# Weight remainders by an accumulating DMA instead of a VectorE subtraction, in a two-layer fp32 trunk

## The chip, the core and the metric

The kernel runs on one core of one Trainium2 chip. The metric is the time of one execution on the device in microseconds, as the median of the runs. Beside it stands one execution taken by the hardware profiler, from which all rows below come.

## The reference, cut to what matters

A two-layer backbone over 256 latent tokens `x` and 256 context tokens `ctx`, 1024 channels wide. Each layer is a half-step SwiGLU feed-forward block, a token mixer of four parallel branches (gated MLP, convolution, bidirectional mLSTM, pooling) with a gated merge, and a second feed-forward block. Shift, scale and gate of each step come from `w_ada`. In the last layer the context is dropped once the mixer has read it.

```python
def swiglu_ffn(h, w_in, w_out):
    a = h @ w_in
    return (jax.nn.silu(a[..., :D_FF]) * a[..., D_FF:]) @ w_out

for l in range(DEPTH):
    ...
    x = residual(x, swiglu_ffn(modulate(x, mod_x, 0), ffn_w_in[l, 0], ffn_w_out[l, 0]), ...)
    h_ctx = residual(h_ctx, swiglu_ffn(modulate(h_ctx, mod_c, 0), ...), ...)
    ...
    y_x, _, _ = token_mixer(modulate(x, mod_x, 1), lw, st_f, st_b)
    x = residual(x, y_x, mod_x, 1, ln_g[l, 1], ln_b[l, 1], 1.0)
    x = residual(x, swiglu_ffn(modulate(x, mod_x, 2), ffn_w_in[l, 1], ffn_w_out[l, 1]), ...)
```

All weights and activations are fp32, and the products have to come out close to fp32.

## The kernel before, in words

Channels lie on the 128 partitions and tokens in the columns: columns 0 to 255 are the context, 256 to 511 the latent tokens, so most matmuls are 512 columns wide, and 256 wide once only the latent tokens are left (second mixer for the most part, and the last feed-forward block).

Each fp32 product is made of three matmuls in a shorter format (`F32R`). A value is split into a high part `hi`, the value rounded to that format, and a remainder `lo`, the value minus `hi`. `mm3` then issues `hi`·`xh`, `hi`·`xl` and `lo`·`xh` into one PSUM tile, in this order: the remainder of a weight is first wanted at the third matmul of a chunk.

`wload` brings in one chunk of weights. SyncE's queue loads it from HBM into a buffer `raw` (128 partitions x 1024 fp32, 512 KiB; 768 columns and 384 KiB for the first part of each feed-forward block's `ffn_out`). `split` has ScalarE write `hi` (line 129) and VectorE write `lo` as `raw` minus `hi` (line 130). There are four `raw` buffers, six `hi` and six `lo`. The `raw` buffers are shared with the rows of `w_ada` (`mods`, line 213, and `start`, line 350), of which VectorE makes two dot products each. `wload` serves the feed-forward blocks (`ffn_tiles`, `out_tiles`), and through `chunk` all projections and the merge of the mixer. Two chunks are split by calls of `split` of their own and not through `wload`: one pair of the first chunks (line 520) and the small gate weights (line 896).

A feed-forward block goes over 22 column blocks in three parts (`PARTS`): for each block two chunks of `ffn_in`, a SiLU on ScalarE, a product on VectorE and a split of the result; after each part eight chunks of `ffn_out` (768 columns wide in the first part). Between the steps of a part, `pump` inserts dot products for the modulation of later steps (`PUMPS`): up to three dot products for each column block or output chunk, none in the last feed-forward block. The mixer inserts work of its branches between projections by the costs that `counted` and `mm` add up.

The engines' instructions are ordered by the tile framework from data dependences and free buffers, so a chunk may be loaded and split before the program text comes to it, as far as buffers are free. GpSimd has some additions at the start (line 375) and memsets of the edges of padded tiles.

Of the kernel before, what the change touches and what calls it, by code (L numbers as in the profile page):

```python
# [10 lines left out]
F32 = mybir.dt.float32  # L11
F32R = mybir.dt.float32r
AF = mybir.ActivationFunctionType
ALU = mybir.AluOpType
# [46 lines left out]
def trunk_kernel(ctx: ExitStack, tc: tile.TileContext, I: dict, out: bass.AP):  # L61
# [11 lines left out]
    def nm(s):  # L73
        uid[0] += 1
        return f"{s}{uid[0]}"
# [27 lines left out]
    V, S, G_ = nc.vector, nc.scalar, nc.gpsimd  # L103
# [6 lines left out]
    def counted(f, fix, per):  # L110
        def g(*a, **k):
            work["v"] += fix + per * size(k["out"] if "out" in k else a[0])
            return f(*a, **k)  # L113
        return g

    tt, stt = (counted(f, 70, 1.05) for f in (V.tensor_tensor, V.scalar_tensor_tensor))
    ts, scan = counted(V.tensor_scalar, 70, 0.55), counted(V.tensor_tensor_scan, 70, 1.05)
# [6 lines left out]
    def act(o, i, f, **kw):  # L124
        S.activation(o, i, f, **kw)  # L125

    def split(hi, lo, src, scale=None):
        if scale is None:
            act(hi, src, AF.Copy)
            tt(out=lo, in0=src, in1=hi.bitcast(F32), op=ALU.subtract)  # L130
        else:
            act(hi, src, AF.Copy, scale=scale)
            stt(out=lo, in0=src, scalar=scale, in1=hi.bitcast(F32), op0=ALU.mult, op1=ALU.subtract)

    def wload(ap, n=1024):
        raw = wp.tile([128, 1024], F32, tag="raw", name=nm("raw"), bufs=4)
        nc.sync.dma_start(raw[:, :n], ap)
        hi = wp.tile([128, 1024], F32R, tag="hi", name=nm("hi"), bufs=6)
        lo = wp.tile([128, 1024], F32R, tag="lo", name=nm("lo"), bufs=6)
        split(hi[:, :n], lo[:, :n], raw[:, :n])  # L140
        return hi, lo

    def mm3(ps, wh, wl, xh, xl, start, stop):
# [359 lines left out]
    def ffn_tiles(l, w, js):  # L503
        tiles = []
        for j in js:
            for h in range(2):
                wh, wl = wload(I["ffn_in"][l, w, j, h])
                tiles.append((mmb(), wh, wl))
        return tiles
# [14 lines left out]
    def ffn(l, w, bd, first, cs, order, np_, nm_=1):  # L524
# [5 lines left out]
        for pi, (j0, j1) in enumerate(PARTS):  # L530
# [26 lines left out]
            def evac(m, p, c, vs):  # L557
                resid(m, p, l, s, vs)
                if fin:
                    nrm.arrive(m, c)  # L560
                pump(nm_)

            rest = out_tiles(lambda m: wload(I["ffn_out"][l, w, m, :, j0 * 128:j1 * 128], (j1 - j0) * 128),
                             gh, gl, cs, order, evac, LAG if fin and len(order) > 1 else 0)
        return nrm, rest
# [8 lines left out]
    def mixer(l, bd, cs, sets, order):  # L574
# [46 lines left out]
        def chunk(key):  # L621
            n = plan.index(key)
            for x in plan[n:n + 1 + AHEAD]:
                if x not in ready:
                    w = I["w_" + x[0]][l]
                    w = w[x[1] // 4, x[1] % 4] if x[0] == "br" else w[x[1]]
                    if plain(x):
                        ready[x] = wp.tile([128, 1024], F32, tag="raw", name=nm("raw"), bufs=4)
                        nc.sync.dma_start(ready[x], w)
                    else:  # L630
                        ready[x] = wload(w)
            pump()
            return ready[key]
# [688 lines left out]
```

## Time and profile before

| | |
|---|---|
| median of 3 runs | 2267.71 us (2266.44 to 2270.55) |
| the profiled execution's own time | 2267.27 us |
| its span | 2265.5 us, 31565 instructions |
| TensorE busy | 2221.0 us (98%) |
| VectorE busy | 1630.0 us (72%) |
| ScalarE busy | 947.0 us (42%) |
| GpSimd busy | 19.9 us (1%) |
| loads, SyncE's queue | 321.22 MB, 43.9% of 16 engines' span |

The span runs from the first to the last instruction; the run's own time has a little around it. Busy time is that in which an engine executed an instruction; the DMA share is the mean busy share of the core's 16 DMA engines. In the rows, `out<-in` names tiles of the program without their buffer numbers, and a line such as L113 or L122 may be a helper's, which records all operations of its kind.

### The profile page before, as it was taken

The numbers are of one execution on the slowest core, as the hardware profiler recorded it, in microseconds if no ns is written. First come the engines' busy times: TensorE is split into PE (matmuls) and PEld (weight loads), VectorE is DVE, ScalarE is ACT, GpSimd is POOL, SyncE is SP. The second block draws the span as 40 slices with busy tenths as digits, with TensorE's granted clock in tenths as the row PEclk, the third lists the DMA queues.
The fourth block names the chain that finished last, engine by engine and source line by source line (L and its number), as shares of the span: only waits on it lengthen the run. The fifth ranks groups of instructions, "written<-read, shape, count | busy, mean of one in ns | idle before, by whom it ended". The sixth has DMA issues, their size and how long they took to land.

```text
span 2265.5 us, 31565 instructions
## 1 busy us (share of the span) xinstructions
PE 2221.0 (98%) x12216; PEld 1908.4 (84%) x12216; DVE 1630.0 (72%) x2881; ACT 947.0 (42%) x1477; POOL 19.9 (1%) x82
## 2 busy tenths in 40 slices
PE   7999999999999999999999999999999999998997
PEld 4888788988888888898888888888889998998997
DVE  6998855768995754795746498766558988776656
ACT  5323123742345753362222254222226645755443
POOL 2000000000000000000000000000000000000000
PEclk9999999999999999999999999999999999999999
DMA  8676643223232132244545425554434543354652
GB/s 308 220 229 221 192 152 94 98 84 113 94 99 88 57 103 93 96 135 150 170 129 158 130 84 186 179 180 152 140 102 142 192 139 103 122 174 136 203 180 83
DMA packets 94454, 323.23 MB, mean 143 GB/s; under 512 B 10592, under 2 KB 12640, under 8 KB 94304
## 3 DMA queue, kind: packets, MB, share of 16 engines
q1 hardware_dynamic: 94304, 321.22, 43.9%
q8 instruction: 96, 1.57, 0.3%
q14 instruction: 54, 0.44, 0.1%
HBM read 320.12 MB, written 1.05 MB: 142 GB/s over the span
## 4 chain that ended last, share of the span: by engine, by line
PE 87%; DVE 7%; DMA 3%; issue 2%; ACT 2%; SPq 0%; DVEq 0%; ACTq 0%
PE mm L122 82%; DVE junk L216 2%; DMA ada<-in_wada 1%; DVE lo L113 1%; PE num L122 1%; DMA raw<-in_ffn_in 1%; DVE junk L366 1%; ACT hi L125 1%; DVE ah L113 0%; PE gt L122 0%; PE ax L122 0%; PE qk L122 0%; PE bcm L122 0%; PE bcr L122 0%; PE st L122 0%
## 5 line engine op out<-in xcount | busy, mean ns | idle before, releaser
L125 ACT ACTIVATE hi<-raw 128x1024 fp32r<-128x1024 f32 (+1 forms) x462 | 474.5, 1031 | 1040.0 <-PE mm L122 659.1
L122 PE MATMUL mm<-xh,hi 128*128 128x512 f32 (+1 forms) x2448 | 847.8, 349 | 5.0 <-ACT hi L125 3.0
L122 PE MATMUL mm<-xl,hi 128*128 128x512 f32 (+1 forms) x2448 | 850.0, 348 | 0.0
L122 PE MATMUL mm<-xh,lo 128*128 128x512 f32 (+1 forms) x2448 | 850.0, 348 | 0.0
L113 DVE TENSOR_TENSOR lo<-raw,hi 128x1024 fp32r<-128x1024 f32 (+1 forms) x462 | 546.2, 1185 | 264.6 <-ACT hi L125 262.4
L122 PEld LDWEIGHTS mm<-xh,hi 128*128 128x128 f32 x2448 | 462.4, 190 | 65.0 <-ACT hi L125 4.4
L122 PEld LDWEIGHTS mm<-xh,lo 128*128 128x128 f32 x2448 | 464.8, 190 | 58.8 <-DVE lo L113 0.4
L122 PEld LDWEIGHTS mm<-xl,hi 128*128 128x128 f32 x2448 | 465.2, 190 | 57.9 <-issue 0.7
L122 PE MATMUL mm<-gh,hi 128*128 128x512 f32 (+1 forms) x1600 | 405.8, 344 | 5.6 <-ACT gh L125 4.7
L216 DVE CUSTOM_DVE_ANT_0 junk<-ada,cbc 128x1024 bf16<-128x1024 f32 x256 | 312.9, 1222 | 107.1 <-DMA ada<-in_wada 104.0
L122 PEld LDWEIGHTS mm<-gh,hi 128*128 128x128 f32 x1600 | 276.6, 189 | 48.0 <-ACT gh L125 5.1
L122 PE MATMUL mm<-gh,lo 128*128 128x512 f32 (+1 forms) x800 | 275.5, 345 | 0.0
L122 PEld LDWEIGHTS mm<-gh,lo 128*128 128x128 f32 x800 | 150.8, 189 | 20.2 <-issue 0.7
L113 DVE SCALAR_TENSOR_TENSOR ah<-mm,gate,ah 128x256 f32<-128x256 f32 x192 | 86.4, 479 | 81.4 <-PE mm L122 81.2
L113 DVE SCALAR_TENSOR_TENSOR cacc<-pd,cw,cacc 128x512 f32<-128x512 f32 (+1 forms) x240 | 133.1, 613 | 0.2
L122 PE MATMUL mm<-yh,hi 128*128 128x512 f32 (+1 forms) x512 | 129.3, 339 | 0.1
L113 DVE TENSOR_TENSOR sg<-sg,mm 128x512 f32<-128x512 f32 (+1 forms) x87 | 53.7, 618 | 82.4 <-PE mm L122 81.7
L122 PEld LDWEIGHTS mm<-yh,hi 128*128 128x128 f32 x512 | 88.0, 189 | 11.6 <-ACT yh L125 0.3
L122 PE MATMUL mm<-yh,lo 128*128 128x512 f32 (+1 forms) x256 | 86.5, 338 | 0.0
L125 ACT ACTIVATE gh<-sg 128x512 fp32r<-128x512 f32 (+1 forms) x88 | 50.5, 574 | 76.0 <-DVE sg L113 75.5
L122 PE MATMUL mm<-mh,hi 128*128 128x256 f32 (+1 forms) x320 | 67.0, 306 | 0.5 <-ACT mh L125 0.3
L125 ACT ACTIVATE xf<-ah,bp,gp 128x256 f32<-128x256 f32 x88 | 48.8, 592 | 21.6 <-DVE ah L113 16.5
(241 smaller groups left out, 1759.6 us busy)
## 6 DMA issues: line engine op xcount, KB each, us to landing
raw<-in_ffn_in SPq DMA_DIRECT2D x176, 512.0 KB, 3.4
ada<-in_wada SPq DMA_DIRECT2D x136, 512.0 KB, 4.2
raw<-in_ffn_out SPq DMA_DIRECT2D x64, 512.0 KB, 3.7
raw<-in_w_G SPq DMA_DIRECT2D x64, 512.0 KB, 3.3
raw<-in_w_br SPq DMA_DIRECT2D x32, 512.0 KB, 3.3
raw<-in_ffn_out SPq DMA_DIRECT2D x32, 384.0 KB, 3.4
raw<-in_w_o SPq DMA_DIRECT2D x24, 512.0 KB, 3.4
shw<-in_wshift SPq DMA_DIRECT2D x16, 256.0 KB, 5.8
```

The lines of the kernel that those rows point to most:

```text
L113: return f(*a, **k)
L122: nc.tensor.matmul(o, w, x, **kw)
L125: S.activation(o, i, f, **kw)
L216: V.tensor_tensor_reduce(out=cur["junk"], in0=w, in1=cur["c"][:, v], scale=1.0, scalar=0.0, op0=ALU.mult, op1=ALU.add, accum_out=m[:, v, t ...
L366: V.tensor_tensor_reduce(out=cur["junk"], in0=w, in1=cur["c"][:, v], scale=1.0, scalar=0.0, op0=ALU.mult, op1=ALU.add, accum_out=m[:, v, k ...
```

## The change: what it does

In `wload` alone, the call of `split` is replaced by three instructions: ScalarE writes `hi` as before, VectorE multiplies `hi` by -1 into `lo`, and GpSimd's queue issues a DMA that adds `raw` to `lo` in place, both in SBUF. The other uses of `split` stay.

```diff
         nc.sync.dma_start(raw[:, :n], ap)
         hi = wp.tile([128, 1024], F32R, tag="hi", name=nm("hi"), bufs=6)
         lo = wp.tile([128, 1024], F32R, tag="lo", name=nm("lo"), bufs=6)
-        split(hi[:, :n], lo[:, :n], raw[:, :n])
+
+        act(hi[:, :n], raw[:, :n], AF.Copy)
+        ts(out=lo[:, :n], in0=hi[:, :n].bitcast(F32), scalar1=-1.0, scalar2=None, op0=ALU.mult)
+        G_.dma_start(lo[:, :n], raw[:, :n], accum_op=ALU.add)
         return hi, lo
```

`act` is an activation on ScalarE, `ts` a `tensor_scalar` on VectorE, `G_` is GpSimd. Nothing else in the kernel differs.

## Rows read from the trace of the kernel before

**Rows 1.** The page: busy times, DMA queue, and the chain that ended last
```profile
PE 2221.0 (98%) x12216; PEld 1908.4 (84%) x12216; DVE 1630.0 (72%) x2881; ACT 947.0 (42%) x1477; POOL 19.9 (1%) x82
...
q1 hardware_dynamic: 94304, 321.22, 43.9%
...
PE 87%; DVE 7%; DMA 3%; issue 2%; ACT 2%; SPq 0%; DVEq 0%; ACTq 0%
```

**Rows 2.** Windows, stages A to G: busy time per engine, clock, DMA share, GB/s
```profile
0.00:300.00 300.00, 281.47 (x1200) 219.60 (x1201) 252.18 (x426) 96.72 (x138) 12.05 (x18) 0.98 0.70 230
300.00:985.00 685.00, 683.65 (x3438) 571.01 (x3438) 481.11 (x873) 306.31 (x493) 4.05 (x35) 1.00 0.29 95
985.00:1675.00 690.00, 689.58 (x3276) 575.89 (x3276) 450.11 (x725) 225.03 (x315) 0.13 (x1) 1.00 0.47 149
1675.00:1760.00 85.00, 84.86 (x639) 79.72 (x638) 71.62 (x145) 50.51 (x93) 0.73 (x10) 1.00 0.40 134
1760.00:1880.00 120.00, 115.83 (x815) 108.53 (x815) 111.67 (x218) 64.75 (x97) 2.25 (x8) 1.00 0.50 161
1880.00:2060.00 180.00, 171.90 (x1263) 161.63 (x1264) 142.37 (x314) 110.94 (x207) 0.67 (x10) 0.96 0.43 137
2060.00:2232.00 172.00, 171.84 (x1418) 171.09 (x1418) 98.60 (x132) 83.76 (x123) 0.00 (x0) 0.99 0.55 172
```

**Rows 3.** The same windows for tile lo alone: PE, PEld, DVE, POOL
```profile
0.00:300.00 300.00, 140.25 (x357) 67.89 (x357) 61.18 (x52) 0.00 (x0) 0.98 0.70 230
300.00:985.00 685.00, 374.68 (x1014) 190.57 (x1014) 134.65 (x114) 0.95 (x1) 1.00 0.29 95
985.00:1675.00 690.00, 403.11 (x1079) 202.70 (x1079) 155.69 (x131) 0.00 (x0) 1.00 0.47 149
1675.00:1760.00 85.00, 58.14 (x199) 37.52 (x198) 23.18 (x19) 0.00 (x0) 1.00 0.40 134
1760.00:1880.00 120.00, 80.63 (x265) 50.05 (x265) 41.86 (x38) 0.95 (x1) 1.00 0.50 161
1880.00:2060.00 180.00, 104.06 (x354) 68.08 (x354) 55.97 (x46) 0.00 (x0) 0.96 0.43 137
2060.00:2232.00 172.00, 134.13 (x473) 90.95 (x473) 71.34 (x61) 0.00 (x0) 0.99 0.55 172
```

**Rows 4.** Groups of VectorE by form: count, busy us, mean ns, idle before
```profile
L113 DVE TENSOR_TENSOR lo<-raw,hi 128x1024 fp32r<-128x1024 f32 x422 | 514.5, 1222 | 250.1 <-ACT hi L125 248.0
L113 DVE TENSOR_TENSOR lo<-raw,hi 128x768 fp32r<-128x768 f32 x32 | 30.6, 955 | 14.5 <-ACT hi L125 14.4
L113 DVE TENSOR_SCALAR lf<-lf,cols 64x512 f32<-64x512 f32 x2 | 0.9, 474 | 0.0
L113 DVE TENSOR_SCALAR gate<-gate 128x16 f32<-128x16 f32 x4 | 0.7, 174 | 0.1
```

**Rows 5.** Windows, the first 57 us, columns as in Rows 2
```profile
0.00:57.00 57.00, 43.87 (x175) 25.73 (x176) 39.45 (x79) 30.33 (x58) 12.05 (x18) 0.97 0.87 306
```

**Rows 6.** Waits of SyncE's queue: us in total, times, longest
```profile
SPq L137 <- DVE lo L113: 1167.1, 304, 20.8
```

**Rows 7.** Tile raw: durations in ns (min/median/max), and its loads' landing
```profile
L125 ACT ACTIVATE hi<-raw x462: 213/1061/1101, 21.3 to 2234.2; 128x1024 fp32r<-128x1024 f32 x142, 128x768 fp32r<-128x768 f32 x10, 128x32 fp32r<-128x32 f32 x2
...
L137 SPq DMA_DIRECT2D raw<-in_ffn_in x174: 327/328/328, 12.5 to 2201.2; - x174
...
DMA to landing us min/median/max: 2.1/3.4/7.7
```

**Rows 8.** Waits of ScalarE, the longest in total
```profile
ACT hi L125 <- PE mm L122: 659.1, 228, 7.1
```

**Rows 9.** Timeline of TensorE at the start: start, duration, the first matmul with lo
```profile
24.38 0.63 PE L122 MATMUL mm<-xh,lo 128*128 128x512 f32 x1
```

**Rows 10.** Stage A for tile ada alone: VectorE busy (x), clock, DMA share
```profile
0.00:300.00 300.00, 151.53 (x122) 0.98 0.70 230
```

## The prediction

> **What bounds the kernel now.** I read the page's busy shares first. TensorE is busy 98% of the span and the chain of work that ended last is 87% TensorE; GpSimd is nearly empty [rows 1]. So little is there to be won (2265.5 - 2221.0 = 44.5 us), and the question is what the change can make TensorE wait for.
>
> Then I cut the span into stages and read the windows, because the change adds transfers and the DMA share differs by stage [rows 2]. A is the start and most of the first feed-forward block, where modulation rows (`ada`) stream in beside the weights: DMA 0.70, VectorE 252 of 300 us. B is the rest of that block and the first mixer: DMA 0.29. C is two feed-forward blocks: 0.47. D, E and F are the second mixer on 256 columns, G the last feed-forward block on 256 columns, where a weight chunk is used up about twice as fast: 0.40, 0.50, 0.43 and 0.55. The same windows for the tile `lo` alone say how many remainders fall in each stage [rows 3].
>
> Last I read what surrounds a chunk. The copy `hi` on ScalarE waits mostly for a TensorE matmul, which frees a `hi` buffer [rows 8]: with six buffers, remainders are made up to five chunks ahead of their use. SyncE's loads wait 1167 us in all for a `lo` subtraction, which frees a `raw` buffer [rows 6]. These are cushions in the steady stages: a remainder that comes a few microseconds later isn't itself a stall there.
>
> **The change, part by part.** `wload` makes 422 + 32 = 454 remainders by a subtraction of 1.222 or 0.955 us [rows 4]; the eight small ones of the gate weights stay as they are. Each subtraction becomes three things.
>
> VectorE's negation: no such row exists at 1024 columns. The nearest with one source in SBUF are 474 ns at 512 columns and 174 ns at 16 [rows 4], a slope of 300/496 = 0.605 ns per column, so 0.174 + 1008 x 0.605 ns = 0.78 us, and 0.63 us at 768. Bounds: 0.47 us (if further columns cost nothing) and 1.22 us (as the subtraction). I take 0.78: VectorE is spared 422 x 0.44 + 32 x 0.32 = 196 us. With TensorE at 98% I cost this at zero; what it could give is a rival below. `hi` is unchanged.
>
> The issue from GpSimd's queue: 454 issues enter a queue that is empty today [rows 1]. An issue waits for its negation, and behind it in the queue stand later issues and the small memsets of the padded tiles, for which ScalarE's copies into those tiles wait. Chunks are made in the order of their use, so I take this wait as hidden by the chunks made ahead. What an issue costs GpSimd no row shows: at the least SyncE's 0.33 us [rows 7], at the most unknown. It sets the pace only if it is longer than TensorE takes for a chunk, 690/131 = 5.3 us in C and 172/61 = 2.8 us in G [rows 2, 3]; I take it as shorter, so it costs nothing.
>
> The transfer, the term that decides. 422 x 512 KiB + 32 x 384 KiB = 234 MB are moved from SBUF into SBUF, on top of 321 MB of loads that hold the engines 43.9% of the span [rows 1]. Price of a load: in the busiest stretch the engines move 306 GB/s at a share of 0.87 [rows 5], so 512 KiB take 524,288 B / 306 GB/s x 0.87 = 1.49 us of all engines; I use 1.5. A load reads a byte and writes it; an accumulate has to read the chunk and the old `lo` and write the sum. No row shows one. Lower bound: 1.5 us, as a load (less is out: the same bytes at least are written). Upper bound: 7.7 us, the slowest landing of any chunk, as if it held all engines throughout [rows 7]. I take 3.0, two reads for one; the median landing, 3.4 us [rows 7], lies beside it.
>
> The Trainium skill (Collectives: The Full Stack, "The bandwidth ceiling: the fold count and why AG ≠ RS ≠ AR") says that adding in the DMA path costs what the second source read costs, with a measured ratio of 1.93. No row of before shows an accumulating transfer. By that ratio an accumulate would be 2.9 us and the sum below 223 instead of 258 us, an estimate.
>
> Now demand against time. Per stage: DMA share x window + accumulates x 3.0 (2.25 for the 384 KiB ones: eight for each feed-forward block's first part, so 8 in A, 16 in C, 8 in G; four small gate remainders, which aren't transfers, come off the counts of B and E) [rows 2, 3].
> A: 210 + 44 x 3.0 + 18 = 360 against 300: +60.
> B: 199 + 110 x 3.0 = 529 against 685: fits.
> C: 324 + 115 x 3.0 + 36 = 705 against 690: +15.
> D: 34 + 19 x 3.0 = 91 against 85: +6.
> E: 60 + 34 x 3.0 = 162 against 120: +42.
> F: 77 + 46 x 3.0 = 215 against 180: +35.
> G: 95 + 53 x 3.0 + 18 = 272 against 172: +100.
> Sum +258 us. It assumes that the loads of a stage can't be moved into another, which four `raw` buffers ensure: a load can be at most four chunks early.
>
> The first chunk has no cushion. TensorE's first matmul with `lo` starts at 24.38 [rows 9], and it runs in order, so that all behind it is as late as this `lo`. The negation saves 0.4 us; an accumulate that lands like a load does so 2.1 to 7.7 us after its issue [rows 7], 4.9 us if the second read adds 1.5 to the median. Other work on TensorE is moved too, and the bounds are 2 and 7 us; I take +4, once.
>
> One wait takes another's place: a `raw` buffer was free when the subtraction ended, and will be when the accumulate has read it. What is late next is SyncE's load into that buffer, then `hi`, and TensorE only when the chunks ahead are used up. At 3.0 us this delay runs beside the shortage of the engines and isn't added.
>
> Sum against the profiled execution: span 2265.5, around it 2267.27 - 2265.5 = 1.8 us; 2265.5 + 258 + 4 + 1.8 = 2529 us. That execution is 0.4 us under the median shown, 2267.71, so nothing is corrected: **2530 us**.
>
> Its own range: if the engines can't be filled beyond the 0.87 of the busiest stretch, each demand is divided by 0.87 and the sum is A 114, C 120, D 20, E 66, F 67, G 141: +528, 2800 us. If instead shares overstate what is taken, because a load at low traffic only waits longer, and the engines can carry a third more than 306 GB/s (400), loads cost by their bytes and an accumulate 2.6 us: about +80, 2350 us.
>
> **Rivals.**
> *An accumulate costs what a load costs (1.5 us).* Then only G is short, 95 + 53 x 1.5 + 9 = 184 against 172: +12, with the start 2283 us; at a ceiling of 0.87 A, E and G give 28, 8 and 39, so 2346 us. For it: half the packets' source is SBUF and not HBM. Against: three streams for two. The Trainium skill (DMA: Bandwidth & Descriptors, "Anatomy of one DMA — SWDGE (gpsimd) path") gives 2.0 us fixed plus bytes at 436 GB/s for a transfer from this queue, an estimate of 1.2 us of moving for 512 KiB, with no word on accumulating; it would place the time here. No row here shows it.
>
> *Faster: the transfers hide and VectorE's relief counts.* In E and F VectorE is busy 112 of 120 and 142 of 180 us while TensorE stands idle 4.2 + 8.1 = 12.3 us [rows 2]. If these gaps are VectorE's and close, 2267 - 12 = 2255 us. It decides only if G holds: (172 - 95)/59 chunks = 1.3 us per accumulate, below a load's price, and the start's wait stays away.
>
> *Buffers, not engines.* A `raw` buffer is held for load, copy (1.06 us), negation and accumulate. With load 3.4 and accumulate 7.7 that is 12.9 us; G: 61 x 12.9/4 = 197 us, +25. With both at 7.7 it is 17.2: G +91, A (with 122/2 = 61 `ada` rows [rows 10], held 7.7 + 2.45) +79, E +27, F +18: +215. So 2296 to 2486 us, say 2390, with a DMA share well below 0.9. For it: loads already wait for `raw` [rows 6]. Against: B and C have room.
>
> *Dearer than two reads.* If the adder or the row-by-row turn-round makes 4.5 us: A 135, B 9, C 206, D 35, E 93, F 104, G 189 = +770, 3041 us; at 7.7 us some 4460. DMA would bound everywhere. Nothing in the rows speaks for it, nothing excludes it.
>
> **How the numbers follow.** Forecast 0.50; as a load 0.18; buffers 0.10; dearer 0.16; faster 0.06. The range: of the faster and as-a-load cases about 0.10 lies below 2280, of the dearer ones 0.10 above 3040, so 2280 to 3040 us; the likeliest alone has 2350 to 2800. A measurement here tells 0.2% (4.5 us) from no change. Faster 0.06; within 0.2% 0.04, a part of the as-a-load case; slower 0.90.
>
> **What would show it.** The accumulates' queue should hold the engines twice as long per byte as the loads' queue; DMA share at 0.9 or more in A, E, F, G; TensorE and its weight loads waiting for the accumulate into `lo`, G longest in proportion; B nearly unchanged in length; the negation at 0.78 us; SyncE's loads waiting for accumulates and not for VectorE. The prediction is wrong if the new queue takes 1.5 us or less per chunk (then 2283), if shares stay at 0.7 while `raw` is waited for (then buffers), if B too becomes long (dearer), or if GpSimd's issue itself takes longer than TensorE's 2.8 to 5.3 us for a chunk.

## The result, and the profile after

The changed kernel takes 2691.28 us (median of 4 runs, 2683.09 to 2702.09) against 2267.25 us: a ratio of 1.1877, 95% interval 1.1855 to 1.1899. Forecast were 2530 us, 2280 to 3040, slower with a chance of 0.90. The sign and the price of a transfer came out as forecast. The loss is 424 us where 263 were forecast.

The page of the changed kernel: busy times, the DMA queues (packets, MB, share of 16 engines' span), and the chain that ended last by engine and by line.

```profile
PE 2332.6 (87%) x12216; PEld 1970.5 (73%) x12216; DVE 1404.2 (52%) x2881; ACT 934.8 (35%) x1469; POOL 419.7 (16%) x536
...
q0 software_dynamic: 65376, 233.86, 47.7%
q1 hardware_dynamic: 94304, 321.22, 34.6%
...
DMA 44%; PE 31%; issue 10%; DVE 10%; ACT 3%; POOL 1%; SPq 0%; POOLq 0%; ACTq 0%; DVEq 0%
PE mm L122 27%; DMA lo<-raw 21%; DMA ada<-in_wada 9%; DMA raw<-in_ffn_out 5%; DMA raw<-in_ffn_in 5%; DVE junk L219 3%; DVE lo L113 2%; ACT hi L125 2%; DVE ah L113 1%; DMA raw<-in_w_G 1%; PE num L122 1%; DMA raw<-in_w_br 1%; POOL lo L143 1%; DMA raw<-in_w_k 1%; DMA raw<-in_w_Au 1%
```

TensorE, 87% of the chain before [rows 1], is 31% of it now, and transfers 44%. The price follows from the queues: the accumulates hold the engines 0.477 x 2690.6 = 1283 us for 233.86 MB, 2.88 us per 512 KiB; the loads 0.346 x 2690.6 = 931 us for 321.22 MB, 1.52 us. The ratio is 1.89. (These shares are times that packets took, summed over the queues. They can add up to more than 1, as the last section shows.)

The tile `lo` in the changed kernel (durations in ns, min/median/max, then first and last start):

```profile
L122 PE MATMUL mm<-xh,lo x2448: 277/389/797, 29.4 to 2639.5; 128*128 128x512 f32 x113, 128*128 128x256 f32 x76
...
L113 DVE TENSOR_SCALAR lo<-hi x454: 549/693/786, 22.5 to 2660.5; 128x1024 fp32r<-128x1024 f32 x142, 128x768 fp32r<-128x768 f32 x10
L143 POOL DMA_DIRECT2D lo<-raw x454: 859/869/1765, 23.5 to 2661.8; - x152
...
DMA to landing us min/median/max: 3.9/6.4/12.1
```

The negation is 0.69 us, the issue on GpSimd 0.87 us, and an accumulate lands 6.4 us after its issue. The first matmul with `lo` starts 5.0 us later than before [rows 9].

To compare stages I cut both spans at the same events, taken from the tile views: the first matmul of `st` (end of the first feed-forward block), the first of `mh` (end of the first mixer's merge), the last of `gt` (gates of the second mixer) and the last of `mh`. The windows between them, columns as in [rows 2], first of the kernel before:

```profile
0.00:398.00 398.00, 379.47 (x1681) 302.01 (x1681) 304.20 (x504) 125.82 (x176) 12.18 (x19) 0.99 0.62 201
398.00:927.00 529.00, 528.07 (x2579) 437.86 (x2578) 375.85 (x687) 248.40 (x402) 3.93 (x34) 1.00 0.28 92
927.00:1816.00 889.00, 888.01 (x4698) 759.63 (x4697) 630.97 (x1088) 339.56 (x512) 2.70 (x13) 1.00 0.46 147
1816.00:2049.00 233.00, 226.53 (x1641) 212.61 (x1641) 188.38 (x396) 134.74 (x236) 1.08 (x16) 0.98 0.43 137
2049.00:2266.00 217.00, 198.91 (x1624) 196.25 (x1623) 130.59 (x210) 98.43 (x152) 0.00 (x0) 0.95 0.47 146
```

and of the changed kernel:

```profile
0.00:495.00 495.00, 402.18 (x1680) 310.38 (x1681) 272.43 (x504) 124.75 (x176) 69.48 (x87) 0.91 0.85 231
495.00:1030.00 535.00, 529.37 (x2579) 437.76 (x2578) 332.54 (x688) 242.34 (x397) 78.74 (x115) 1.00 0.74 175
1030.00:2112.00 1082.00, 947.34 (x4712) 795.11 (x4711) 558.01 (x1131) 337.45 (x517) 158.91 (x195) 0.93 0.81 203
2112.00:2384.00 272.00, 233.32 (x1633) 218.11 (x1631) 140.19 (x343) 127.64 (x224) 54.42 (x75) 0.92 0.93 226
2384.00:2691.00 307.00, 220.36 (x1619) 209.14 (x1618) 101.00 (x218) 102.62 (x158) 58.16 (x66) 0.88 0.91 221
```

Before, the five stretches took 398, 529, 889, 233 and 216 us (the last window above runs half a us past the span's end), so the loss is 97, 6, 193, 38 and 91 us. Two things are to be seen. The DMA share is 0.91 to 0.93 only in the last two stretches; in the long middle one it is 0.81, and yet this one loses most. And TensorE is busy 2332.6 us for the same 12216 matmuls that took 2221.0: where it stood idle the granted clock fell (0.91, 0.93, 0.92, 0.88 in the stretches with stalls, 1.00 in the first mixer; its lower level is 1.2 of 2.4 GHz), and I read the longer busy time as that clock's: the first mixer, at 1.00 in both kernels, has 529 us of it against 528, the middle, at 0.93 against 1.00, has 947 against 888. It is 112 of the 425 us of span; 313 are idle time.

Why the middle loses with engines to spare shows in the chain of the changed kernel, in order of time, in this stretch (start, us, what):

```profile
1302.21 7.79 DMA raw<-in_ffn_out
...
1310.10 1.07 ACT hi L125
...
1311.19 0.70 DVE lo L113
...
1312.82 5.38 DMA lo<-raw
...
1318.24 6.57 DMA ada<-in_wada
...
1324.83 1.23 DVE junk L219
...
1328.13 0.61 DVE lo L113
...
1329.37 4.53 DMA lo<-raw
```

A load lands, its copy and negation follow, the accumulate frees the `raw` buffer, a modulation row is loaded into it, VectorE takes its dot products, and only then comes the next negation. The timelines of ScalarE (the copy for it) and of VectorE (the first dot product, the negation) in the same stretch:

```profile
1318.12 1.06 ACT L125 ACTIVATE hi<-raw 128x1024 fp32r<-128x1024 f32 x1 [4.50 <-PE mm L122]
...
1324.83 1.23 DVE L219 CUSTOM_DVE_ANT_0 junk<-ada,cbc 128x1024 bf16<-128x1024 f32 x1 [10.48 <-DMA ada<-in_wada]
...
1328.04 0.68 DVE L113 TENSOR_SCALAR lo<-hi 128x1024 fp32r<-128x1024 f32 x1
```

The copy had ended at 1319.18, so the negation came 8.9 us late. VectorE had stood idle for 10.48 us before the dot products, for whose row it waited, and the negation stood behind them in its order. The waits say the same of the whole span: SyncE's queue, which waited for subtractions [rows 6], now waits for accumulates, VectorE for modulation rows, and TensorE for accumulates and for `gh`, the product inside a feed-forward block, which VectorE and ScalarE make.

```profile
SPq L137 <- DMA lo<-raw: 1738.7, 366, 21.5
SPq L217 <- DMA lo<-raw: 318.0, 74, 9.2
...
PE mm L122 <- DMA lo<-raw: 133.4, 74, 6.3
PE mm L122 <- ACT gh L125: 114.6, 17, 14.6
...
DVE lo L113 <- ACT hi L125: 642.5, 228, 10.2
DVE junk L219 <- DMA ada<-in_wada: 403.9, 81, 10.5
```

### The profile page after: what moved, and what is told of

It reads as the page before. It is cut to its first block, busy times and chain, and to the rows that moved or that the text cites. A ratio compares the mean times of both kernels' runs of the same rounds, so it can differ in the third digit from the quotient of the medians.

```text
span 2690.6 us, 32716 instructions
## 1 busy us (share of the span) xinstructions
PE 2332.6 (87%) x12216; PEld 1970.5 (73%) x12216; DVE 1404.2 (52%) x2881; ACT 934.8 (35%) x1469; POOL 419.7 (16%) x536
## 3 DMA queue, kind: packets, MB, share of 16 engines
q0 software_dynamic: 65376, 233.86, 47.7%
q1 hardware_dynamic: 94304, 321.22, 34.6%
## 4 chain that ended last, share of the span: by engine, by line
DMA 44%; PE 31%; issue 10%; DVE 10%; ACT 3%; POOL 1%; SPq 0%; POOLq 0%; ACTq 0%; DVEq 0%
PE mm L122 27%; DMA lo<-raw 21%; DMA ada<-in_wada 9%; DMA raw<-in_ffn_out 5%; DMA raw<-in_ffn_in 5%; DVE junk L219 3%; DVE lo L113 2%; ACT hi L125 2%; DVE ah L113 1%; DMA raw<-in_w_G 1%; PE num L122 1%; DMA raw<-in_w_br 1%; POOL lo L143 1%; DMA raw<-in_w_k 1%; DMA raw<-in_w_Au 1%
## 5 line engine op out<-in xcount | busy, mean ns | idle before, releaser
L122 PE MATMUL mm<-xh,lo 128*128 128x512 f32 (+1 forms) x2448 | 875.4, 358 | 112.5 <-DMA lo<-raw 112.3
L122 PE MATMUL mm<-xh,hi 128*128 128x512 f32 (+1 forms) x2448 | 867.0, 356 | 13.9 <-DVE sg L113 5.7
L122 PE MATMUL mm<-xl,hi 128*128 128x512 f32 (+1 forms) x2448 | 866.0, 354 | 0.0
L143 POOL DMA_DIRECT2D lo<-raw x454 | 403.5, 894 | 2203.9 <-DVE lo L113 1334.1
L113 DVE TENSOR_SCALAR lo<-hi 128x1024 fp32r<-128x1024 f32 (+1 forms) x454 | 309.1, 682 | 643.9 <-ACT hi L125 642.5
L122 PEld LDWEIGHTS mm<-xh,lo 128*128 128x128 f32 x2448 | 478.2, 195 | 191.7 <-DMA lo<-raw 132.9
L122 PE MATMUL mm<-gh,hi 128*128 128x512 f32 (+1 forms) x1600 | 433.6, 361 | 126.2 <-ACT gh L125 114.6
L122 PEld LDWEIGHTS mm<-xh,hi 128*128 128x128 f32 x2448 | 477.7, 196 | 74.7 <-DVE sg L113 7.0
L122 PEld LDWEIGHTS mm<-gh,hi 128*128 128x128 f32 x1600 | 292.5, 199 | 182.1 <-ACT gh L125 121.4
L122 PEld LDWEIGHTS mm<-mh,hi 128*128 128x128 f32 x320 | 55.6, 205 | 10.1 <-ACT mh L125 6.4
```

The lines of the kernel that those rows point to most:

```text
L122: nc.tensor.matmul(o, w, x, **kw)
L143: G_.dma_start(lo[:, :n], raw[:, :n], accum_op=ALU.add)
```

## The experiments

Two theories stood against each other. *Engines*: the added transfers fill the 16 DMA engines, and the loss is demand beyond the time of a stage. *Buffers*: four `raw` buffers, held until the accumulate has landed, and VectorE's order run a chain that sets the pace while the engines have room. Each kernel was timed against the kernel before on the same chip. The tile framework orders the instructions anew for each kernel, so differences of a few us in a stage aren't read.

**Less in the transfer.** Four kernels keep the change and alter only the line that issues the accumulate. They leave additions out, so they no longer compute the layer; only their times are read.

```diff
 e1_half
-        G_.dma_start(lo[:, :n], raw[:, :n], accum_op=ALU.add)
+        G_.dma_start(lo[:, :n // 2], raw[:, :n // 2], accum_op=ALU.add)
 e2_cols32
+        G_.dma_start(lo[:, :32], raw[:, :32], accum_op=ALU.add)
 e3_copy
+        G_.dma_start(lo[:, :n], raw[:, :n])
 e4_nodma: the line is left out
```

> The accumulate adds only the left half of each chunk (512 of 1024, 384 of 768 columns); the right half of each remainder keeps the negated high part. Negation, issue, waits and buffers stay. Engines theory (the added transfers fill the 16 DMA engines): 1.44 us per chunk instead of 2.88, every stage fits but the last feed-forward block (95 + 85 against 172), so 2275 to 2290 us. Buffers theory (four raw buffers, held until the accumulate has landed, run a chain load - copy - negation - accumulate - next load): the landing falls only from 6.4 to about 4.5 us, so most of a third of the loss goes, 2400 to 2500 us, with a DMA share near 0.65 and SyncE's loads still waiting for accumulates over 1000 us.

> The accumulate adds only 32 columns (4 KiB of each 512 KiB is 3%): practically no bytes, but the same issues, waits and landings; the remainders are wrong beyond column 32. Engines theory: back to the time before, 2260 to 2275 us. Buffers theory: the landing stays at 2.5 us or more and the issue at 0.9 us, a raw buffer is held some 3 us longer than before, a loss of 20 to 100 us remains: 2290 to 2370 us.

> The same transfer from GpSimd's queue without the addition: raw is copied over lo, so the remainder is the whole chunk. Same bytes written, one read fewer per byte. Two-reads theory: the queue holds the engines about 1.5 us per 512 KiB instead of 2.88; time as for the half accumulate, 2275 to 2290 us if engines are the limit, 2400 to 2500 us if buffers are. If the price lies in this queue or in SBUF as source and not in the second read, the queue stays near 2.9 us per 512 KiB and the time near 2690 us.

> No transfer at all: the remainder is the negated high part, made at 0.69 us instead of 1.22 us. The raw buffer is free as soon as ScalarE has copied it. Both theories: no loss, 2250 to 2267 us. What it is below 2267 is all that VectorE's relief can give; if that is under 5 us, the relief was worth nothing measurable.

| | median us | ratio to before (95%) | queue 0 per 512 KiB moved | landing, median |
|---|---|---|---|---|
| e1_half | 2435.58 | 1.0747 (1.0718 to 1.0775) | 3.07 us | 4.8 us |
| e2_cols32 | 2302.09 | 1.0162 (1.0147 to 1.0178) | | 2.4 us |
| e3_copy | 2406.05 | 1.0617 (1.0596 to 1.0638) | 1.51 us | 4.3 us |
| e4_nodma | 2259.48 | 0.9976 (0.9966 to 0.9986) | | |

Queue 0 of the copy, and its issue on GpSimd:

```profile
q0 software_dynamic: 65376, 233.86, 28.1%
```
```profile
L143 POOL DMA_DIRECT2D lo<-raw x454: 527/527/1022, 23.6 to 2368.5; - x152
```

0.281 x 2396.8 us over 233.86 MB is 1.51 us per 512 KiB: a copy from this queue, SBUF to SBUF, costs what a load costs, and the addition 1.91 times that. So the price is the addition's and not the queue's. No run parts the second read from the adding itself. Nor is it a matter of full engines: the 92 accumulates of h2 below, where there was room, took 0.120 x 2259.2 us over 48.24 MB, 2.95 us per 512 KiB.

```profile
q0 software_dynamic: 13248, 48.24, 12.0%
```

The times speak for buffers. The half accumulate was to cost next to nothing if engines were the limit (2275 to 2290); it cost 170 us, with shares of 0.69 in the middle and 0.80 in the last stretch. Practically without bytes there is still a loss of 36 us: the landing of 2.4 us and the issue alone lengthen the hold. All of it lies in the first and the middle stretch (419 and 914 us, 21 and 25 more than before), which are the ones with modulation rows; the last two took 222 and 216. And without any transfer the kernel gains 6.6 us, the whole worth of VectorE's relief and of buffers that come free at the copy.

**Cutting the chain with the full accumulate kept.**

```diff
 f1_raw6: wherever raw is allocated, for weights and modulation rows
-        raw = wp.tile([128, 1024], F32, tag="raw", name=nm("raw"), bufs=4)
+        raw = wp.tile([128, 1024], F32, tag="raw", name=nm("raw"), bufs=6)
-    bp = ctx.enter_context(tc.tile_pool(name="bp", bufs=33))
+    bp = ctx.enter_context(tc.tile_pool(name="bp", bufs=32))
 f2_ada2: both places of modulation rows; raw stays at 4, bp at 32
-            w = wp.tile([128, D], F32, tag="raw", name=nm("ada"), bufs=4)
+            w = wp.tile([128, D], F32, tag="ada", name=nm("ada"), bufs=2)
 f3_actneg
-        ts(out=lo[:, :n], in0=hi[:, :n].bitcast(F32), scalar1=-1.0, scalar2=None, op0=ALU.mult)
+        act(lo[:, :n], hi[:, :n].bitcast(F32), AF.Copy, scale=-1.0)
 f4_before6: the kernel before with the edits of f1_raw6
```

> The changed kernel with six raw buffers in place of four (one work tile of 33 given up for the space). Buffers theory: each load may start two chunks earlier, the hold of a buffer no longer sets the pace where the engines have room; what is left is the demand on the engines, which by the measured 2.88 us per accumulate makes 2490 to 2590 us; DMA share 0.85 or more. Engines theory (0.82 of the share is all they give beside two queues): 2660 to 2700 us.

> The changed kernel with four raw buffers for weights alone and two of their own for the modulation rows (the same space as six). Cuts the link accumulate - load of a modulation row - VectorE's dot products, which exists in the first block and the two in the middle. If that link carries the middle's loss: the two middle blocks come back to within 60 us of before, total 2530 to 2610 us, the last block unchanged at some 300 us. If not: 2650 us or more.

> The changed kernel with the negation on ScalarE, right behind the copy, and none on VectorE. In the trace of the changed kernel a negation stands up to 9 us behind dot products that wait for a modulation row. If VectorE's order is a link of the chain that costs: 2590 to 2660 us. If only buffers and engines count, 2680 to 2710 us.

> Control: the kernel before with six raw buffers and one work tile less. Both theories: its loads waited for buffers only off the critical chain, except in the first 300 us; 2255 to 2270 us.

f1_raw6 took 2587.62 us (1.1423, 1.1404 to 1.1443), f2_ada2 2634.20 (1.1609, 1.158 to 1.1639), f3_actneg 2586.74 (1.1414, 1.1393 to 1.1435), f4_before6 2260.37 (0.9973, 0.9962 to 0.9983). More buffers and the negation off VectorE take some 104 us each, the latter slightly more than expected; both are links. The bytes and the price are the same in all three, so what they took off wasn't demand. f1_raw6 came out at the upper edge of what was expected, and its DMA share, 0.84, below the 0.85 or more that was expected with it.

By stretch the two mends differ. f3_actneg took 454, 541, 1017, 264 and 312 us: it gains 41 us in the first and 65 in the middle, where the modulation rows are, 8 in the fourth and nothing in the last. f1_raw6 took 480, 531, 1045, 252 and 279 us: it gains in every stretch, 48 us of it in the last two, so these weren't free of the chain either.

f2_ada2 was a partial miss: 2634 lies above the expected 2610, and the middle took 1007 us, not within 60 of before (889). Of the 75 us that it gained there, 32 stand in the first mixer, which took 567 us instead of 535: part of the dot products had moved into it (VectorE ran 817 instructions there instead of 688). Over both stretches f2_ada2 took 43 us off and f1_raw6 41, so two buffers for the rows alone did there what two for any load did. The last two stretches have no rows and gained 5 us by f2_ada2; that the last stayed near 300 us (299) was as expected.

**The floor.** g1 has both mends. g2 is the kernel before with its subtraction, and beside it the same traffic into two scratch tiles of 512 KiB that nothing reads (for their space, one work tile of 33 less):

```diff
 g2_traffic
         split(hi[:, :n], lo[:, :n], raw[:, :n])
+        scr.reverse()
+        G_.dma_start(scr[0][:, :n], hi[:, :n].bitcast(F32), accum_op=ALU.add)
```

> Both mends at once: negation on ScalarE and six raw buffers, the full accumulate kept. Each alone took about 104 us off. If they cut two links of one chain and the demand on the engines is the floor: 2490 to 2550 us with a DMA share of 0.88 or more. If the two gains add up, 2480 us; if they are the same gain twice, 2570 to 2590 us.

> The kernel before, subtraction kept, and beside it an accumulate of each high part into a scratch tile that nothing reads: the same bytes, price and queue, but neither a raw buffer nor TensorE waits for it. Engines theory (what is lost is the engines' time): most of the loss without its chain, 2450 to 2550 us. Buffers theory (what is lost is the chain through the buffer): 2275 to 2400 us, longest in the last block, with the same share per accumulate.

g1_actneg_raw6 took 2499.16 us (1.103, 1.1011 to 1.1048), g2_traffic 2489.42 us (1.0988, 1.0971 to 1.1004). Windows between the same events as above, all but the first mixer, first of g1:

```profile
0.00:447.00 447.00, 391.37 (x1679) 306.54 (x1680) 231.13 (x436) 190.59 (x244) 68.62 (x87) 0.94 0.92 259
...
980.00:1967.00 987.00, 918.39 (x4714) 780.06 (x4713) 470.49 (x995) 514.10 (x709) 155.46 (x195) 0.96 0.87 224
1967.00:2215.00 248.00, 227.40 (x1629) 213.27 (x1627) 90.12 (x247) 175.41 (x269) 52.23 (x75) 0.97 0.95 239
2215.00:2496.00 281.00, 214.90 (x1620) 202.68 (x1618) 60.14 (x149) 163.40 (x221) 56.34 (x65) 0.94 0.93 239
```

and of g2:

```profile
0.00:445.00 445.00, 388.58 (x1687) 303.59 (x1689) 305.65 (x506) 125.35 (x176) 70.09 (x87) 0.95 0.92 258
...
975.00:1935.00 960.00, 902.77 (x4695) 767.71 (x4694) 624.33 (x1079) 335.76 (x511) 154.70 (x194) 0.97 0.89 228
1935.00:2200.00 265.00, 231.38 (x1647) 216.30 (x1645) 190.73 (x401) 133.69 (x235) 49.61 (x72) 0.95 0.92 233
2200.00:2488.00 288.00, 216.15 (x1618) 209.60 (x1618) 131.10 (x214) 100.26 (x154) 58.96 (x68) 0.87 0.96 235
```

Two quite different kernels with the same bytes end within 10 us of each other, with shares of 0.87 to 0.96 outside the first mixer. The two gains of 104 us nearly add up (2691 - 2 x 104 = 2483). So 2691 - 2499 = 192 us of the loss are chain, at least: the same bytes cost that much less with the chain eased. The 224 to 233 us that are left are what full engines cost at the most. That they are full engines alone isn't shown. The two kernels differ by 27 us in the middle and by 17 and 7 the other way in the last two stretches; g1's share over the span is 0.86, below the 0.88 or more that was expected of the floor; a share near these isn't full by itself (from 1100 to 1200 us g2's TensorE was busy all 100 us at a share of 0.94); and g2 has waits of its own, its `hi` copies 193 us for the scratch transfers.

**Half the bytes without the chain, and the accumulate where there is room.** h1 is g1 with the half accumulate of e1. h2 is f4_before6 with the accumulate (negation on VectorE) only while the first mixer is built:

```diff
 h2_mixer0
+    by_dma.append(1)
     nrm, rest = mixer(0, bd, full, (0, 1), order)
+    by_dma.clear()
```

> The half accumulate (left half of each chunk only) with the chain cut: negation on ScalarE, six raw buffers. With the old chain it took 2436 us. If that loss was the chain and not the engines: the demand by the measured 1.53 us per half chunk overfills only the last block, by some 13 us, so 2275 to 2300 us. If something else beside the chain cost it: 2340 us or more.

> The accumulate only for the chunks of the first mixer, where the engines have room (0.28 before) and no modulation rows are loaded; the subtraction everywhere else; six raw buffers. If the loss belongs to full engines and the chain alone, it is free here: 2255 to 2268 us, no change against the kernel before with six buffers (2260), and VectorE's relief gives nothing there because TensorE is busy 99.8% of that stage. If an accumulate costs something by itself, 2275 us or more.

h2_mixer0 took 2262.20 us (0.9988, 0.9978 to 0.9998), as expected: 92 accumulates where the engines have room cost nothing that can be told from f4_before6, and win nothing.

h1_half_cut was a miss: 2342.51 us (1.0341, 1.0314 to 1.0369) instead of 2275 to 2300. The last two stretches came back as expected, 219 and 224 us (233 and 216 before); the first lost 29 and the middle 54, and these are the ones with modulation rows.

```profile
958.00:1901.00 943.00, 909.37 (x4714) 776.80 (x4713) 470.61 (x996) 514.45 (x709) 155.49 (x195) 0.97 0.70 187
```
```profile
DVE junk L219 <- DMA ada<-in_wada: 290.9, 87, 9.1
```

The share in the middle is 0.70, so full engines aren't what it lost by. VectorE's dot products wait 291 us for modulation rows (104 us before the change), and these loads still wait for `raw` buffers that accumulates hold. I read it as the chain's remaining link, through the modulation rows and VectorE's order to the products behind them; e2_cols32 and f3_actneg point the same way, since what the one lost and the other gained lies in the stretches with rows. But no run took that link alone out with the other two gone, and the six `hi` and six `lo` buffers stayed six in every run, so this stays argued. It also means that g1's 2499 us may hold some chain.

## Why the prediction came out as it did

*The price.* Right: 3.0 us was taken, 2.88 measured, against 1.52 for a load; that it is the second read's, as the prediction had it, no run shows. The lower bound, 1.5 us, is what e3_copy measured for a copy. The Trainium skill's ratio in Collectives: The Full Stack ("The bandwidth ceiling: the fold count and why AG ≠ RS ≠ AR"), 1.93, agrees with the 1.89 and 1.91 of these runs. With 2.88 us in the prediction's own terms the sum is 54 in A, 0 in C, 4 in D, 38 in E, 30 in F and 93 in G, +219 in place of +258. The total is near what g1 and g2 lost, +224 to +233, but that is in part luck, since the split doesn't fit. The first stretch does (47 and 49 us against 54). In the middle, where the terms give some 20 us (C, D and half of E), g1 lost 98 and g2 71 us; in the last, against 93 in G, 65 and 72. What was too little in one place and too much in another cancels.

*The step that failed* is the one on the `raw` buffer: "At 3.0 us this delay runs beside the shortage of the engines and isn't added." It is added. Its term was nothing, and the mends that shorten the delay and leave the bytes took 192 us off. The prediction had counted the buffers as a rival to full engines, worth up to 215 us, with the rival's mark a share well below 0.9. Both were there at once: between the profiled executions of the changed kernel and of g1, 95 us of the gain lie in the middle (share 0.81), 48 in the first stretch and 50 in the last two, which at 0.93 and 0.91 look full.

Against the rival stood "B and C have room". For C this rested on an omission: the working counts modulation rows in A alone, and C has 69 of them (138 dot products).

```profile
985.00:1675.00 690.00, 168.75 (x138) 1.00 0.47 149
```

With the rival's dearest holds C needs (131 x 17.2 + 69 x 10.15)/4 = 738 us of 690. The rival also lacked VectorE's order: a negation waits behind dot products whose row waits for a buffer. That the negation's place on VectorE lengthens the chain, f3_actneg shows.

*The clock* was no term. 112 us of the span are TensorE busy longer with the same matmuls, and they go with the stalls: 46 us in g2 (2266.7 - 2221.0; mean granted clock 0.958), 61 in g1 (0.963), 112 in the changed kernel (0.935, against 0.991 in the kernel before).

*VectorE's relief at zero*: right within 7 us. e4_nodma gains 6.6 us, about half of the faster rival's 12, and f4_before6 gains 5.7 us without touching VectorE, so even this need not be relief. The negation cost 0.69 us (0.78 taken).

*The start*: `lo` came 5.0 us later, 4.5 had been worked out and 4 taken; what it cost isn't told apart, since the first matmuls also stand in another order.

*The first mixer unchanged*: right, 535 against 529 us at a share of 0.74. *GpSimd's issue shorter than a chunk's time*: right, 0.87 us.

Of the kernels here f4_before6 is the fastest one that keeps the whole computation, by 0.27% (0.17 to 0.38) over the kernel before; h2_mixer0 is no faster. No version with accumulates beat it.

## What to carry to other kernels

An accumulating DMA in place of a subtraction trades VectorE's time, which had slack, for DMA time at 1.9 times a load's price, and it must be set against the DMA share of each stage, not of the span. Before calling a later landing hidden, add up how long each buffer is held, from its load to the last reader's landing, and go through every engine's order for what stands behind a wait on that buffer. Full engines and a chain through buffers don't exclude each other: here the chain was worth some 190 us at least and full engines 224 to 233 at most, and a lower granted TensorE clock went with the stalls, on top of the waiting.

## What the runs showed of the hardware that wasn't expected

GpSimd's issue of an accumulate takes 0.87 us whether it moves 512 KiB, 256 KiB or 16 KiB (869 ns median in each), and that of a plain copy 0.53 us. With two queues at work the engines reached shares of 0.89 to 0.96 over whole stretches, above the 0.87 of [rows 5], so that the ceiling of 0.87, from which 2800 us was worked out, was too low. The share isn't bounded by 1 either. In two windows of 100 us of the changed kernel, at the end of the second mixer and in the last block, it reads 1.03 with both queues at work:

```profile
2300.00:2400.00 100.00, 70.75 (x526) 68.57 (x524) 43.07 (x98) 37.89 (x61) 21.19 (x24) 0.84 1.03 257
...
2500.00:2600.00 100.00, 78.61 (x588) 75.48 (x587) 25.37 (x48) 30.75 (x41) 21.78 (x25) 0.91 1.03 255
```

A demand that is added up from shares against a limit of 1, as the prediction's is, has that uncertainty.
